# A hybrid GLA/HGRN2 diffusion step: each burst of the scan ordered behind a mark in the projection work

## The chip, the cores and the metric

The kernel runs on one core of one Trainium2 chip. The core has a matrix engine (TensorE, PE in the profile, with its weight loads as PEld), three engines for elementwise work (VectorE or DVE, ScalarE or ACT, GpSimd or POOL), a queue that issues transfers (SyncE, SP) and 16 DMA engines. Each engine works through its own queue of instructions in order and waits on semaphores for the others. The metric is the device time of one execution in microseconds; the median of several runs counts.

## The reference

One layer of a bidirectional backbone on 128 context tokens and 1024 latent tokens, width 1024, in float32:

```python
h = rmsnorm(x, norm1) * (1 + scale1) + shift1
mix, new_gla, new_hgrn = hybrid_mixer(h, s_gla, s_hgrn, w_in, w_gla_up, b_gla, lb, ...)
x = x + gate1 * mix
h = rmsnorm(x, norm2) * (1 + scale2) + shift2
x = x + gate2 * conv_ffn(h, w_ffn_up, ffn_conv, b_ffn_conv, w_ffn_down, grid)
```

The mixer projects h with `w_in` to queries, keys, values, gates and forget gates of 4 GLA heads (key width 64) and 4 HGRN2 heads (128), runs for each head a gated linear recurrence S_t = diag(f_t) S_{t-1} + k_t v_t^T, o_t = S_t^T q_t forward and backward over the tokens, adds both outputs, normalises them per head, multiplies by silu of a gate and projects with `w_out`. Modulation vectors come from `silu(c) @ w_ada`. The feed-forward part has a 3x3 depthwise convolution over the latent grid. Outputs are the two token tensors and the final states of the context.

## The kernel before

Large products run as three float32r products each (high times high, and the two with one low part), so every weight is split once: ACT writes the high part (`wh`, L127), POOL or DVE subtracts it to get the low part (`wl`, L65).

The first 750 us hold the mixer. The tokens are three blocks of 384; heads come in six groups: groups 0 and 1 are pairs of GLA heads, groups 2 to 5 one HGRN2 head each. Two streams of work share PE:

- *The scan* (`levels`). A block's intra-block scores are made by doubling: on levels 0 to 6 the decayed queries Q and keys k are updated in place by DVE (`update`, L886, L888, L892), ACT makes mixed copies of them (`mixed`, L876), and PE multiplies keys by queries in small 32-column products. One `burst` (L907 to L931) holds the products of two levels: 24 products, or 48 for a GLA pair, chained so that they go one behind the other, in float32, which the trace shows as two records each. A block has four bursts, a group 12, the scan 72. DVE picks the wanted parts of the PSUM result by a mask (`keep`). The next update of Q must wait until the burst has read it.
- *The fill* (`parts`, `all_steps`): all other projections of `w_in` in the order in which the groups need them (`proj_d_steps`, L598, 128 columns of weights against 384 tokens; `proj_t_steps`, L612, values, token-major), 2448 matmuls, and behind them `fill_steps`, the output projection of the first six token tiles over seven of the eight heads (L738, 252 matmuls). The memory of the normalised tokens is given back before `fill_steps`; its weights, the merged heads and a gate (L720) are loaded into that memory.

The main loop (L1185 to L1224) goes over groups, blocks and eight slots a block. Each even slot holds a burst, so a burst has an interval of two slots, and each slot has two parts. In every part the loop traces fill up to a planned number of columns (`goal`, from `GOALS`, with `D_COLS` = 27648 columns for one set of 128 weight columns); this fill is ordered behind the latest burst (`tc.issue_after(last.ins)`), in group 5 behind the latest state or output product (`anchor["mm"]`). In the same slots stand the steps of the block before: key transposes (`keys`, L984), state products (L991), and the outputs of the group before (`out_steps`: L1025 to L1028, L1051, L1065, turned by L1075), and, in groups 2 to 4, the products of the modulation (`ada_product`, L1152), whose weight pieces are loaded one interval ahead. `gates` (L818 to L857) prepares the next block; its `k` tile is one of two buffers.

The order on each queue is not written out: a planner in the framework simulates the engines with its own costs and takes, of the instructions that are ready in its simulation, the one that was traced first. `tc.high_priority(offset=BURST_AHEAD)` puts a burst 1000 instructions ahead in that rank, so a burst is taken as soon as its operands are ready there. `tc.issue_after(x)` adds an edge: the instructions traced in the block come behind x on x's engine, without waiting for its end. PSUM tiles of the fill (`ps_mm`) come in two buffers.

Behind the scan, from about 750 us, come the rest of the output projection, the feed-forward part with its convolution, and the down projection. The change does not touch them.

Of the kernel before, what the change touches and what calls it, by code (L numbers as in the profile page):

```python
# [49 lines left out]
def kernel(ctx: ExitStack, tc: tile.TileContext, ins, outs, stop=None):  # L50
# [9 lines left out]
    mm = nc.tensor.matmul  # L60

    anchor = {}
# [321 lines left out]
    for i in range(2):  # L384
        nc.vector.memset(modA[i], 0.0)
        t = modA[i][:, :]
# [7 lines left out]
    for i in range(2):  # L394
        ps = (ps_a, ps_mm)[i].tile([2 * 32, 512], F32, name="ada", tag=("ada", "mm")[i])
        psA.append(ps)
        for kt in range(KT):
# [4 lines left out]
            for j in range(2):  # L402
# [4 lines left out]
                    start=(kt == 0),  # L407
                    stop=(kt == KT - 1),
# [85 lines left out]
    def proj_d(w, b):  # L494

        hi, lo = w
        ps = ps_mm.tile([P, BL], F32, name="mm", tag="mm")
        n = 0
        for kt in range(KT):
            for a, h in ((hi, h1h), (hi, h1l), (lo, h1h)):  # L500
                mm(ps, a[:, kt, :], h[kt][b], start=(n == 0), stop=(n == 23))
                n += 1
        return ps

# [86 lines left out]
    def proj_d_steps(w, b, done):  # L591

        hi, lo = w
        ps = ps_mm.tile([P, BL], F32, name="mm", tag="mm")
        n = 0
        for kt in range(KT):
            for a, h in ((hi, h1h), (hi, h1l), (lo, h1h)):
                mm(ps, a[:, kt, :], h[kt][b], start=(n == 0), stop=(n == 23))  # L598
                n += 1
            if kt == KT - 1:  # L600
                done(ps)
            yield 3 * BL

    def proj_t_steps(w, t, done):

        ps = ps_mm.tile([P, 2 * P], F32, name="mm", tag="mm")
        ts_ = slice(t % 3 * P, (t % 3 + 1) * P)
        n = 0
        for kt in range(KT):
            hi, lo = w[kt // 4]  # L610
            for h, a in ((h1h, hi), (h1h, lo), (h1l, hi)):
                mm(ps, h[kt][t // 3][:, ts_], a[:, kt % 4, :], start=(n == 0), stop=(n == 23))  # L612
                n += 1
            if kt == KT - 1:
                done(ps)
            yield 3 * 2 * P
# [58 lines left out]
    def fill_steps():  # L675
# [14 lines left out]
        ws = list(next_ws(3))  # L690
# [32 lines left out]
        for b in range(2):  # L723
            if b == 1:
                ms = [load_merged(b, p) for p in range(3)]
            ms.append(load_merged(b, 3))
            for i in range(3):
                t = 3 * b + i
                xs = flat(vp.tile([P, NTILE, P], F32, name="v", tag="v"))
                nc.sync.dma_start(xs[:, 0:D], x_src(t))  # L730
                ts_ = slice(i * P, (i + 1) * P)
                for half in range(2):
                    cs = slice(half * 512, (half + 1) * 512)
                    ps = ps_mm.tile([P, 512], F32, name="mm", tag="mm")
                    for f in range(7):
                        for n, (a, wi) in enumerate(((0, 0), (0, 1), (1, 0))):
                            lhs = ms[f // 2][:, f % 2, a, ts_]
                            mm(ps, lhs, ws[f][wi][:, cs], start=(f + n == 0), stop=(f == 6 and n == 2))  # L738
                        if f == 6:
                            e = evp.tile([P, 512], F32, name="ev", tag="ev")  # L740
                            nc.vector.tensor_tensor(e, ps, gate[:, cs], op=ALU.mult)
                            nc.vector.tensor_tensor(e, e, xs[:, cs], op=ALU.add)
                            nc.gpsimd.dma_start(scr_pre[t][:, cs], e)
                        yield 3 * 512
                if t == 0:

                    cv = ins["ffn_conv"].rearrange("o a b (k p) -> (o a b k) p", p=P)
                    cr = flat(vp.tile([P, NTILE, P], F32, name="v", tag="v"))
                    nc.sync.dma_start(
                        cr[0:99, 0:512].rearrange("r (i p) -> r i p", i=4), cv.rearrange("(i r) p -> r i p", i=4)  # L750
                    )
                if t == 2:
                    for j in range(4):
                        pt = ps_x.tile([P, 512], F32, name="x", tag="x")
                        nc.tensor.transpose(pt[:, 0:99], cr[0:99, j * P : (j + 1) * P], ident[0:99, 0:99])
                        nc.vector.tensor_copy(conv_c[0][:, 99 * j : 99 * j + 99], pt[:, 0:99])
                if t == 4:
                    pos["end"] = n_in + 4
                    w_late.update({1: ws[1], 2: ws[2], 7: next_w()})
# [99 lines left out]
    def levels(u, b, fb, k, k0):  # L859
# [47 lines left out]
        def burst(*parts):  # L907

            widths = [LB << max(lev - NLOW, 0) for lev, _, _ in parts]
            pss = [ps_lv.tile([P, 3 * sum(widths)], F32, name="lv", tag="lv") for _ in u.heads]  # L910
            strips, at = [], 0
            for w in widths:
                strips.append([ps[:, at : at + 3 * w].rearrange("p (i n) -> p i n", i=3) for ps in pss])
                at += 3 * w
            last = None
            with tc.high_priority(offset=BURST_AHEAD):
                for (lev, keys, src), got in zip(parts[::-1], strips[::-1]):
                    for i in range(3):
                        for j in range(P // LB):
                            js = slice(j * LB, (j + 1) * LB)  # L920
                            for ps, (r0, r1) in zip(got, u.heads):
                                with tc.issue_after(last.ins) if last is not None else nullcontext():
                                    last = mm(  # L923
                                        ps[js, i, :],
                                        keys[r0:r1, i * P + j * LB : i * P + (j + 1) * LB],
                                        queries(lev, src, i, j, r0, r1),
                                        start=True,
                                        stop=True,
                                        skip_group_check=True,
                                    )  # L930
            return strips, last  # L931
# [182 lines left out]
    class Steps:  # L1114
# [12 lines left out]
        def drain(self):  # L1127
            while self.next is not None:
                self.step(self.next[0])
# [44 lines left out]
    def stream(goal, after):  # L1174
        nonlocal streamed
        while streamed < goal:
            with tc.issue_after(after.ins) if after is not None else nullcontext():
                got = next(steps, None)
            if got is None:
                return  # L1180
            streamed += got
# [3 lines left out]
    for n, u in enumerate(groups):  # L1185
        if not u.gla:
            u.v = [u.vpair[u.hd % 2]]
        if n == 0:
            start_group(u)
            ready = gates(u, 2)  # L1190
        for bi, b in enumerate(ORDER):
            fb, k, k0 = ready
            lv = levels(u, b, fb, k, k0)
            for slot in range(8):
                at = 8 * bi + slot
                last = anchor["mm"] = next(lv)
                if 2 <= n < 5 and slot % 2 == 0:
                    with tc.issue_after(last.ins):
                        with tc.high_priority(offset=BURST_AHEAD):
                            ada_product()  # L1200
                        ada_load()
                with tc.issue_after(last.ins):
                    outs_.step("half", at)
                    states.step("product")
                if slot == 5 and (b > 0 or n < 5):
                    if b > 0:
                        ready = gates(u, b - 1)
                    else:
                        start_group(groups[n + 1])
                        ready = gates(groups[n + 1], 2)  # L1210
                for part in range(2):
                    with tc.issue_after(last.ins):
                        if part == 0:
                            states.step("keys")
                        outs_.step("full", at)
                        if part == 1:
                            outs_.step("full", at)
                    goal = GOALS[n] + (GOALS[n + 1] - GOALS[n]) * (16 * bi + 2 * slot + part + 1) / 48
                    stream(goal, None if n == bi == 0 else anchor["mm"] if n == 5 else last)
            drain(lv)  # L1220
            states.drain()
            states = Steps(state_steps(u, b, k))
        outs_.drain()
        outs_ = Steps(out_steps(u))  # L1224
# [801 lines left out]
```

## Time and profile before

| | us |
|---|---|
| median of 3 runs | 1598.65 |
| lowest, highest | 1595.45, 1601.4 |
| profiled execution | 1602.16 |
| its span on the core | 1600.4 |
| PE busy | 1513.8 |
| DVE busy | 1160.1 |
| ACT busy | 793.1 |
| POOL busy | 726.4 |
| first and last burst start | 96.86, 688.97 |

The profiled execution is one run of the program under the hardware profiler; its time is 3.5 us above the median. Times inside the trace count from the start of the span. A matmul's record lasts longer than the distance to the next, since matmuls are pipelined: what PE loses shows as a stretch in which no record runs, put down as "idle before" with the engine that ended it. Bursts are counted here from 0 to 71, in the order of PE's queue.

### The profile page before, as it was taken

What the parts mean: (1) busy time and instruction counts of PE and PEld (TensorE: products, weight loads), DVE (VectorE), ACT (ScalarE), POOL (GpSimd) and SP (SyncE); (2) the same over time, 40 slices, a digit from 0 to 9 for tenths busy, and PEclk for the clock granted to TensorE, in tenths of its full rate; (3) what the DMA queues carried; (4) which work ended last, traced back from release to release, by engine and by line L of the source; (5) the groups of instructions that cost most, each with busy time, mean ns of one, the idle gap of its engine ahead of it and who ended that gap; (6) DMA issues with size and microseconds to landing.
All of it is one profiled execution on the core that took longest, in us unless ns stands there. A gap on an engine that the chain in (4) does not pass through costs nothing.

```text
span 1600.4 us, 31095 instructions
## 1 busy us (share of the span) xinstructions
PE 1513.8 (95%) x12506; PEld 1269.1 (79%) x12506; DVE 1160.1 (72%) x1724; ACT 793.1 (50%) x1526; POOL 726.4 (45%) x535
## 2 busy tenths in 40 slices
PE   7999998999999998799868999999999998999997
PEld 2699987989898988677656888888888886788886
DVE  3657563675575576544589999999999999678565
ACT  3566666545454455412664444444444444457444
POOL 1412122242432331201168999999999996200001
PEclk9999999999999999999979999999999999999999
DMA  9211111353544452644721464554554657879752
GB/s 334 100 56 46 38 46 52 104 148 121 168 138 133 141 174 92 257 165 152 259 72 40 132 191 131 135 142 122 176 139 111 186 137 212 320 232 356 254 187 116
DMA packets 164650, 244.61 MB, mean 153 GB/s; under 512 B 11124, under 2 KB 107618, under 8 KB 162586
## 3 DMA queue, kind: packets, MB, share of 16 engines
q1 hardware_dynamic: 142583, 168.54, 32.7%
q0 software_dynamic: 21312, 73.41, 15.1%
q8 instruction: 98, 1.61, 0.4%
q10 hardware_dynamic: 611, 0.68, 0.1%
q14 instruction: 46, 0.38, 0.1%
HBM read 186.95 MB, written 78.71 MB: 166 GB/s over the span
## 4 chain that ended last, share of the span: by engine, by line
PE 49%; DVE 6%; issue 2%; DMA 1%; ACT 1%; POOL 1%; POOLq 0%; SPq 0%; DVEq 0%; ACTq 0%
PE u L1477 25%; PE xb L1888 6%; PE yb L1888 5%; PE x L1682 4%; PE mm L738 3%; PE u L1370 2%; PE yb L1939 2%; DVE acc L1618 2%; PE x L1292 0%; DVE wl L65 0%; DMA scr_m<-hi 0%; DMA wh<-scr_wo 0%; DVE t4l L65 0%; DMA raw<-in_w_ffn_down_dram 0%; DMA mh<-scr_m 0%
## 5 line engine op out<-in xcount | busy, mean ns | idle before, releaser
L1618 DVE SCALAR_TENSOR_TENSOR acc<-u,convc,acc 128x945 f32<-128x945 f32 (+2 forms) x352 | 426.8, 1218 | 8.3 <-ACT acc L1606 1.8
L65 POOL TENSOR_TENSOR wl<-raw,wh 128x1024 fp32r<-128x1024 f32 x42 | 103.0, 2457 | 240.8 <-ACT wh L127 195.0
L598 PE MATMUL mm<-h1h,wh 128*128 128x384 f32 x528 | 185.5, 351 | 0.6 <-DVE g L647 0.6
L598 PE MATMUL mm<-h1h,wl 128*128 128x384 f32 x528 | 181.8, 344 | 0.0
L598 PE MATMUL mm<-h1l,wh 128*128 128x384 f32 x528 | 180.6, 342 | 0.0
L65 POOL TENSOR_TENSOR wul<-sr,wuh 128x512 fp32r<-128x512 f32 (+1 forms) x68 | 123.2, 1814 | 25.3 <-ACT wuh L1463 25.1
L65 POOL TENSOR_TENSOR wul<-ra,wuh 128x1024 fp32r<-128x1024 f32 x46 | 118.8, 2583 | 10.7 <-ACT wuh L1463 7.6
L886 DVE TENSOR_TENSOR Q<-Q,fb 128x384 f32<-128x384 f32 x126 | 80.4, 638 | 57.0 <-PE lv L923 55.6
L876 ACT ACTIVATE m<-k 128x384 f32<-128x384 f32 x126 | 70.2, 557 | 78.3 <-DVE k L888 38.3
L1863 POOL TENSOR_TENSOR sq<-sq,mhalf 128x1 f32<-128x1 f32 x9 | 11.1, 1238 | 213.9 <-DVE sq L1860 213.9
L598 PEld LDWEIGHTS mm<-h1h,wh 128*128 128x128 f32 x528 | 101.0, 191 | 4.3 <-issue 2.6
L598 PEld LDWEIGHTS mm<-h1h,wl 128*128 128x128 f32 x528 | 100.5, 190 | 2.2 <-issue 1.7
L598 PEld LDWEIGHTS mm<-h1l,wh 128*128 128x128 f32 x528 | 100.9, 191 | 1.1 <-issue 0.8
L888 DVE TENSOR_TENSOR k<-k,fb 128x384 f32<-128x384 f32 x126 | 76.4, 606 | 18.3 <-ACT m L876 10.3
L127 ACT ACTIVATE wh<-raw 128x1024 fp32r<-128x1024 f32 x55 | 58.1, 1057 | 54.2 <-DMA raw<-in_w_in_dram 14.8
L612 PE MATMUL mm<-wh,h1h 128*128 128x256 f32 x288 | 83.3, 289 | 0.0
L612 PE MATMUL mm<-wl,h1h 128*128 128x256 f32 x288 | 81.1, 282 | 0.0
L612 PE MATMUL mm<-wh,h1l 128*128 128x256 f32 x288 | 80.9, 281 | 0.0
L1463 ACT ACTIVATE wuh<-ra 128x1024 fp32r<-128x1024 f32 x44 | 46.4, 1054 | 38.0 <-issue 34.0
L1647 ACT ACTIVATE u2p<-u 128x512 f32<-128x512 f32 x44 | 26.3, 598 | 75.0 <-PE u L1477 71.8
L1714 POOL TENSOR_TENSOR acc<-acc,acc 128x1152 f32<-128x1152 f32 x22 | 59.6, 2711 | 6.9 <-DVE acc L1618 6.9
L1463 ACT ACTIVATE wuh<-sr 128x512 fp32r<-128x512 f32 (+1 forms) x66 | 51.0, 773 | 22.2 <-PE x L1682 16.2
(355 smaller groups left out, 4545.0 us busy)
## 6 DMA issues: line engine op xcount, KB each, us to landing
ra<-in_w_ffn_up_dram SPq DMA_DIRECT2D x88, 256.0 KB, 3.0
raw<-in_w_in_dram SPq DMA_DIRECT2D x32, 512.0 KB, 4.7
raw<-in_w_ada_dram SPq DMA_DIRECT2D x32, 512.0 KB, 4.1
scr_g<-acc POOLq DMA_DIRECT2D x22, 576.0 KB, 5.4
scr_s<-late POOLq DMA_DIRECT2D x11, 1024.0 KB, 4.2
scr_t<-in_w_ffn_down_dram POOLq DMA_DIRECT2D x16, 704.0 KB, 7.2
wa<-in_w_ada_dram SPq DMA_DIRECT2D x16, 512.0 KB, 6.4
raw<-in_w_out_dram SPq DMA_DIRECT2D x13, 512.0 KB, 3.6
```

What stands on the lines that cost most here:

```text
L65: return eng.tensor_tensor(out, full, hi.bitcast(F32), op=ALU.subtract)
L598: mm(ps, a[:, kt, :], h[kt][b], start=(n == 0), stop=(n == 23))
L612: mm(ps, h[kt][t // 3][:, ts_], a[:, kt % 4, :], start=(n == 0), stop=(n == 23))
L876: nc.scalar.activation(aps(t, 0, [[2 * h, NB], [h, 2], [1, h]]), aps(src, 0, [[2 * h, NB], [BL + h, 2], [1, h]]), AF.Copy)
L886: nc.vector.tensor_tensor(qm, qm, aps(ff_, 2 * h - 1, [[BL - h, 2], [2 * h, NB], [0, h]]), op=ALU.mult)
L888: nc.vector.tensor_tensor(km, km, aps(ff_, BL + 2 * h - 1, [[-(BL + h), 2], [2 * h, NB], [0, h]]), op=ALU.mult)
L1463: nc.scalar.activation(hi, raw, AF.Copy)
L1477: last = mm(dst, W[x][:, a, kt, :], HB[y][b][:, kt, :], start=(start and n == 0), stop=(stop and n == 11), skip_group_check=True,)
L1618: last = nc.vector.scalar_tensor_tensor(o, u3[:, r0 + dy : r1 + dy, c0 + dx : c1 + dx], wc(3 * (dy + 1) + dx + 1), o, op0=ALU.mult, op1=AL ...
L1682: last = mm(pk, HB[h]["p"][:, 4 * half + kt, :], aps(flat(W[x]), a * 512 + kt * P, [[(b - a) * 512, 2], [1, P]]), start=(half + kt + n == ...
L1714: last = nc.gpsimd.tensor_tensor(accg, accg, accu, op=ALU.mult)
L1888: anchor["down"] = mm(banks[i], w[a][:, ts_], w[b][:, 512:1024], start=(start and j == 0 and n == 0), stop=(j == NPAIR - 1 and n == 2), sk ...
```

## The change

Every matmul of the fill is noted as `anchor["fill"]` when it is traced. In the main loop, after the fill of the first part of an odd slot, which is the third of the four parts of an interval, the last fill matmul traced so far is noted as `anchor["paced"]`. The first product of the next burst, which until now had no ordering edge, is ordered behind that matmul; the other products of the burst are chained to the first as before. The priority of the burst, the fill's own edges and all data are the same.

```diff
@@ proj_d, proj_d_steps, proj_t_steps, fill_steps (each of the four fill matmuls)
-                mm(ps, a[:, kt, :], h[kt][b], start=(n == 0), stop=(n == 23))
+                anchor["fill"] = mm(ps, a[:, kt, :], h[kt][b], start=(n == 0), stop=(n == 23))
...
@@ burst
-            last = None
+            last = anchor.get("paced")
             with tc.high_priority(offset=BURST_AHEAD):
                 for (lev, keys, src), got in zip(parts[::-1], strips[::-1]):
...
@@ main loop
                     goal = GOALS[n] + (GOALS[n + 1] - GOALS[n]) * (16 * bi + 2 * slot + part + 1) / 48
                     stream(goal, None if n == bi == 0 else anchor["mm"] if n == 5 else last)
+                    if slot % 2 == 1 and part == 0:
+                        anchor["paced"] = anchor["fill"]
```

More of the change, by code (lines that the diff above doesn't have):

```diff
@@ L597, in proj_d_steps @@
             for a, h in ((hi, h1h), (hi, h1l), (lo, h1h)):
-                mm(ps, a[:, kt, :], h[kt][b], start=(n == 0), stop=(n == 23))
+                anchor["fill"] = mm(ps, a[:, kt, :], h[kt][b], start=(n == 0), stop=(n == 23))
                 n += 1
@@ L611, in proj_t_steps @@
             for h, a in ((h1h, hi), (h1h, lo), (h1l, hi)):
-                mm(ps, h[kt][t // 3][:, ts_], a[:, kt % 4, :], start=(n == 0), stop=(n == 23))
+                anchor["fill"] = mm(
+                    ps, h[kt][t // 3][:, ts_], a[:, kt % 4, :], start=(n == 0), stop=(n == 23)
+                )
                 n += 1
@@ L737, in fill_steps @@
                             lhs = ms[f // 2][:, f % 2, a, ts_]
-                            mm(ps, lhs, ws[f][wi][:, cs], start=(f + n == 0), stop=(f == 6 and n == 2))
+                            anchor["fill"] = mm(
+                                ps, lhs, ws[f][wi][:, cs], start=(f + n == 0), stop=(f == 6 and n == 2)
+                            )
                         if f == 6:
```

## The prediction

> **What bounds the kernel now.** First the page, then the waits of PE, then single stretches of PE's timeline. The page says PE 95%; the windows view splits the span into the first five groups of the scan, the last group with the tail, and everything behind the scan (length, busy time of PE, PEld, DVE, ACT, POOL, granted clock, DMA share, GB/s).
>
> ```profile
> span 1600.4 us, 31095 instructions
> PE 1513.8 (95%) x12506; PEld 1269.1 (79%) x12506; DVE 1160.1 (72%) x1724; ACT 793.1 (50%) x1526; POOL 726.4 (45%) x535
> 96.86:621.42 524.56, 506.34 (x7224) 464.10 (x7223) 320.77 (x696) 289.01 (x760) 146.92 (x127) 0.99 0.34 105
> 621.42:751.81 130.39, 113.94 (x1128) 95.73 (x1128) 66.80 (x169) 42.43 (x136) 19.56 (x27) 0.96 0.45 160
> 751.81:1600.40 848.59, 809.93 (x3743) 658.43 (x3741) 727.77 (x769) 414.82 (x542) 530.50 (x351) 0.98 0.56 176
> ```
>
> The change acts on the first two stretches. PE does the same matmuls before and after, so the change can only win or lose PE's idle time there: 524.56 - 506.34 = 18.2 us and 130.39 - 113.94 = 16.5 us. The waits view of PE says who ended it (us in total, times, longest); the first three rows are of the first stretch, the others of the whole span.
>
> ```profile
> PE lv L923 <- ACT m L876: 10.1, 5, 5.9
> PE ada L1152 <- DMA raw<-in_w_ada_dram: 4.3, 4, 1.2
> PE x L984 <- DVE st L1003: 2.0, 1, 2.0
> ...
> PE lv L923 <- ACT m L876: 14.9, 8, 5.9
> DVE Q L886 <- PE lv L923: 55.6, 42, 3.2
> ```
>
> L923 is the burst: eight of 72 bursts stop PE because their operand (L876) is late. The last row is the other direction: the scan's own engine waits for bursts, so the scan runs as fast as PE lets it.
>
> **Where the bursts stand now.** The new fence is the fill matmul that is last when the planner has traced three of four parts of an interval. In group n, burst j (0 to 11), the mark is GOALS[n] + (GOALS[n+1]-GOALS[n])*(4j-1)/48 columns, rounded up to a step of three matmuls. For group 2, j=11: 11.5+6.6*43/48 = 17.41 D_COLS; three v parts (216 matmuls each), eleven column parts (72 each) and 0.41*72 = 30 make 1470. The trace gives the fill actually issued: windows from 0 to a burst's start, of L598 alone and of L612 alone (matmul count in the second column).
>
> ```profile
> 0.00:391.54 391.54, 135.80 (x696) 121.33 (x696) 0.97 0.33 105
> 0.00:391.54 391.54, 83.48 (x648) 77.47 (x648) 0.97 0.33 105
> 0.00:272.93 272.93, 77.53 (x396) 68.63 (x396) 0.96 0.31 98
> 0.00:272.93 272.93, 55.75 (x432) 51.72 (x432) 0.96 0.31 98
> 0.00:557.33 557.33, 239.75 (x1241) 214.14 (x1241) 0.98 0.37 116
> 0.00:557.33 557.33, 111.56 (x864) 103.37 (x864) 0.98 0.37 116
> ```
>
> That burst goes at 696+648 = 1344, 126 before its mark. Done for all 72 bursts, 62 stand before their mark (9 to 60 matmuls mostly, up to 126) and move back; ten do not. Among the ten are two first bursts of a block: at 272.93 us the fill is at 828, which is all that is traced ahead of that burst, and at 557.33 at 2105 (mark 2106, limit 2112). So the scan runs ahead inside a block and then stands at the next block's start until the planned fill has caught up; a large stock of fill lies between. The edit takes the head start away and leaves PE at most a quarter interval, 9 to 15 matmuls, of fill that may go ahead of a late burst.
>
> **The change, part by part.** It adds no instruction; 62 ordering edges on PE's queue are what acts. The assignments to the anchor cost nothing. Behind a burst are queued its block's DVE updates and ACT copies, the ada products, the state and output products and the next fill, all fenced by it.
>
> 1. *Bursts that stop PE.*
>
> ```profile
> 212.54 0.77 PE L923 MATMUL lv<-Q,m 64*32 64x32 f32 x44 [1.93 <-ACT m L876]
> 272.93 0.71 PE L923 MATMUL lv<-Q,m 64*32 64x32 f32 x44 [5.91 <-ACT m L876]
> 432.09 0.40 PE L923 MATMUL lv<-Q,m 128*32 128x32 f32 x24 [1.68 <-ACT m L876]
> 656.20 0.34 PE L598 MATMUL mm<-h1l,wh 128*128 128x384 f32 x1
> 656.37 0.34 PE L598 MATMUL mm<-h1h,wl 128*128 128x384 f32 x1
> 212.70:216.11 3.41, 3.41 (x103) 3.35 (x102) 2.42 (x7) 1.89 (x3) 1.09 (x1) 0.50 0.02 5
> 605.23:608.64 3.41, 3.41 (x13) 3.41 (x13) 3.41 (x6) 1.43 (x5) 1.66 (x1) 0.50 0.39 115
> ```
>
> The bursts at 212.54 and 432.09 are 27 and 21 matmuls before their marks. A fill matmul goes every 0.17 us (the two L598 rows), so 4.6 and 3.6 us of fill go ahead of them, more than the 1.93 and 1.68 us they waited: 3.61 us gained. The one at 272.93 already stands at its limit; its 5.91 us stay. The last two rows (windows, granted clock in the third figure from the end) show that a stop also costs clock: 3.41 us at half rate follow the 1.93 us gap, and the same the 2.03 us gap at L984, so removing the first returns another 3.41/2 = 1.7. Term: -5.3 (bounds -5.3 and 0, if another burst inherits the wait).
> The Trainium skill ("TensorE: Matmul & The Clock Gate", Part 1: The HAM clock gate) has the clock fall after at least one idle window of about 3.4 us. By that rule a 1.93 us gap would cost only itself, the term would be -3.6 and the sum 1.7 us later; the row above disagrees, and I take the row.
>
> 2. *Ada products*.
>
> ```profile
> 343.15 0.64 PE L1152 MATMUL ada<-raw,cT 128*32 128x256 f32 x8 [1.23 <-DMA raw<-in_w_ada_dram]
> ```
>
> They (L1152) go right behind a burst and wait 4.3 us in four places for a piece whose load was issued one interval earlier. Even spacing helps where bursts stood close; but the wait shown, the longest, comes behind a burst that is 8.1 us after the one before it. I take half: -2.1 (bounds -4.3 and 0). The L984 gap of 2.0 us ends with a late state evacuation and is not touched: 0 (bounds -3.7 and 0).
>
> 3. *The change of stage in the last group.* Up to now bursts of group 5 fill PE while the output projection (L738) waits for its loads. Its mark for the first burst of block 1 is 2451, three matmuls past the last of the 2448 projection matmuls: that burst now waits for L738's first products, and the next (mark 2469) for the first seven weight pieces.
>
> ```profile
> 656.56 0.33 SPq L142 DMA_DIRECT2D wh<-scr_wo  x1
> 662.27 0.32 SPq L698 DMA_DIRECT2D mh<-scr_m  x1
> DMA  0000039955999999999999200000086030770999
> 669.11 0.48 PE L984 MATMUL x<-ident,k 128*128 128x128 f32 x1 [5.47 <-ACT st L995]
> 656.71:682.33 25.62, 14.89 (x197) 10.66 (x196) 14.45 (x38) 12.56 (x32) 5.39 (x8) 0.87 0.95 369
> 692.27 9.55 PE mm L738 x42
> 689.04 0.66 PE lv L923 x48
> 684.21 1.23 PE L991 MATMUL x<-v,kt 128*128 128x128 f32 x4 [0.89 <-ACT kt L987]
> ```
>
> The loads are issued from 656.56 (the last projection is done at 656.7) to 662.27, and the DMA slices of the window 640 to 715 (1.9 us each) stay full until about 682, 25.6 us later. In that stretch (656.71 to 682.33) PE is idle 25.62 - 14.89 = 10.7 us now, doing bursts, states and 24 L738 matmuls. With the fence it may do some 21 L738 matmuls (0.23 us each by the 42 in 9.55 us: 4.8), one burst (0.66), and gate, turn and state products that I put at 2.6 from the same timeline: 8.1, so 17.5 idle, 6.8 more. The gap of 0.89 us right behind it goes. Term: +6.0. Lower bound -4, if the loads land as fast and the 5.47 us stop, which is behind an ACT queue held by an output's DMA, goes too; upper bound +11.6, a second stop of that size. Behind it L738 is plentiful and PE full again.
>
> 4. *Block starts.*
>
> ```profile
> 551.60 0.27 PE L984 MATMUL x<-ident,k 128*128 128x128 f32 x1
> 552.08 0.52 ACT L852 ACTIVATE k<-fj 128x384 f32<-128x384 f32 x1
> 557.33 0.46 PE L923 MATMUL lv<-Q,m 128*32 128x32 f32 x24
> 426.30 2.88 DVE L864 TENSOR_TENSOR Q<-fb,qj 128x768 f32<-128x768 f32 x1 [2.31 <-ACT qj L510]
> 425.97 2.40 POOL L65 TENSOR_TENSOR wl<-raw,wh 128x1024 fp32r<-128x1024 f32 x1 [3.72 <-ACT wh L127]
> ...
> 607.69 0.56 DVE L888 TENSOR_TENSOR k<-k,fb 128x384 f32<-128x384 f32 x1
> 608.17 0.95 DVE L864 TENSOR_TENSOR Q<-fb,qj 128x768 f32<-128x768 f32 x1
> ```
>
> The first burst of a block follows the last key transpose of the block before last by 5.7 us, because L852 needs that k tile. Now ACT and DVE are free of the scan in that time; afterwards the block's own updates run there. An update is three DVE operations of about 0.56 us (607.69) and two lie in an interval: 3.3 us. Places within 4 matmuls or so of their limit now are few (182.5, 272.9, 557.3, 621.4 us); I take 0.75 us at each: +3.0. Bounds 0 and 4*3.3 = 13.2.
>
> Sum: -5.3 - 2.1 + 6.0 + 3.0 = +1.6 us. The profiled execution took 1602.16 us (span 1600.4), so 1603.8 by its own time; the median of the three runs shown is 3.5 lower, 1598.65, and gives 1600.
>
> **Rivals.** *Faster: the handover costs nothing.* For it: even intervals of (689.0-96.9)/71 = 8.3 us hold the 3.3 us of updates and three ACT copies with room, so a chip that runs later than the planner thought is covered at every burst. Terms: -5.3, -4.3, the L984 gap with its clock -3.7, the others 0: -13.3, 1585. Against it: the loads of the next stage cannot start before 2448 in either order.
> *Slower: PE runs dry at block starts.* With no stock of fill, each of the six starts that stand within 14 matmuls of their limit (118.3, 147.4, 182.5, 272.9, 557.3, 621.4 us) is late by the 3.3 us of updates, less the margin (0, 14, 3, 0, 7, 4 matmuls, 28*0.17 = 4.8): 19.8 - 4.8 = 15.0 in place of 3.0, so 1598.65 + 1.6 + 12 = 1612. It decides from a mean lateness of about 2.5 us a start. The pair of rows at 426 us speaks for it: a DVE step took 2.88 us while POOL was in a split; the same form took 0.95 us at 608.17. Against it: idle time at starts was small where the margin was large.
> The Trainium skill ("SBUF — State Buffer", SBUF: two separate sides) calls the port pair of DVE and GpSimd an exclusive lock, the loser blocked for the whole instruction. That pair of rows agrees.
> *The fence does nothing*: only if bursts already stood behind their marks, and 62 do not. 1599.
>
> **How the numbers follow.** Forecast 1600 (own range 1592 to 1608) 45%, handover free 1585 22%, starts dry 1612 31%, no effect 2%. A measurement tells about 0.5%, 8 us, from no change: below 1590.7 is faster, above 1606.6 slower. The forecast's ends give 3% faster and 5% slower, so 0.27, 0.37 and 0.36. Range 1584 to 1616: from the first rival to a little past the second, where terms 3 and 4 may both be at half their upper bounds.
>
> **What would show it.** Right: nearly all bursts at their marks; the waits PE lv on ACT m lose the 1.93 and 1.68 us entries; no L738 before, and one burst only, between the last projection and some 20 us later; DVE's wait for L923 grows well past 55.6 us. Wrong: the stretch behind the last projection stays at 10.7 us idle or less, the first bursts of blocks show new PE waits of 2 to 3 us at many places, or the stretch behind 751.81 changes length, on which nothing here acts.

## The result, and the profile after

The changed kernel took 1617.8 us (median of four runs, 1616.1 to 1619.2), the kernel before 1598.5 beside it (four runs, 1595.5 to 1601.4): a ratio of 1.0121, with a 95% interval from 1.0099 to 1.0142. It is slower, by 19 us. The prediction said 1600, with a range from 1584 to 1616. The profiled execution of the changed kernel took 1619.2 us, 1.4 above the median.

The head of its page, PE's waits between 180 and 780 us, and one row of DVE's waits (us in total, times, longest):

```profile
span 1617.3 us, 31087 instructions
PE 1514.2 (94%) x12506; PEld 1264.6 (78%) x12506; DVE 1149.6 (71%) x1724; ACT 800.1 (49%) x1530; POOL 727.7 (45%) x535
```

```profile
PE mm L598 <- ACT wh L127: 14.5, 3, 7.2
PE mm L740 <- DMA mh<-scr_m: 12.0, 5, 6.1
PE lv L927 <- ACT on L1039: 7.1, 1, 7.1
PE mm L598 <- POOL wl L65: 4.3, 3, 1.5
...
PE ada L1156 <- DMA raw<-in_w_ada_dram: 1.4, 2, 1.0
...
DVE Q L890 <- PE lv L927: 90.6, 48, 11.4
```

In this kernel L923, L984, L1152 and L738 of before are L927, L988, L1156 and L740; L598 kept its number. PE's busy time is what it was. Of the waits of bursts one long one is left, at k20 (7.1 us). New are the first and the fourth row: the *fill* stops, and it stops on its own weights. (The second row, 1.6 us in one wait before, belongs to the change of stage in the last group.) Twice the high part (ACT, L127) is about 7 us late, and each time the low part (POOL, L65) holds the third matmul another 1.4 us.

The windows view from the first burst to k20 (which in both kernels stands at fill 828), from there to k60 (fill 2345 before, 2349 after), and from k60 to the last fill matmul. First the kernel before, then the changed one; columns as in the prediction.

```profile
96.86:272.93 176.07, 166.89 (x2913) 152.69 (x2912) 103.15 (x246) 109.71 (x280) 33.76 (x27) 0.98 0.15 42
272.93:621.42 348.49, 339.45 (x4312) 311.40 (x4312) 217.62 (x451) 179.31 (x481) 113.16 (x101) 0.99 0.44 137
621.42:751.41 129.99, 113.54 (x1126) 95.42 (x1125) 66.80 (x169) 42.43 (x136) 19.56 (x27) 0.96 0.44 159
```

```profile
94.00:266.71 172.71, 163.24 (x2912) 149.29 (x2912) 102.13 (x244) 113.66 (x276) 32.49 (x25) 0.99 0.15 43
266.71:636.03 369.32, 345.35 (x4315) 314.32 (x4316) 206.19 (x453) 180.87 (x489) 115.60 (x102) 0.96 0.41 129
636.03:767.84 131.81, 115.53 (x1122) 94.33 (x1122) 68.57 (x169) 43.53 (x136) 18.48 (x27) 0.95 0.44 157
```

Up to k20 the changed kernel is 3.4 us faster, in the last group 1.8 slower, and in between it loses 20.8: its idle time there is 369.32 - 345.35 = 24.0 in place of 9.0, and the granted clock falls from 0.99 to 0.96. The sum, 19.3, is the whole loss. (The first burst starts 2.9 us earlier in this execution; it starts between 92.7 and 94.6 us in all the others, whatever their marks, so that is not an effect of the change.)

**What stops the fill.** The first stop on the queues of SP, ACT, POOL and PE (start, duration, and the idle time in brackets):

```profile
319.10 0.62 PE L1156 MATMUL ada<-raw,cT 128*32 128x256 f32 x6
319.75 0.34 SPq L126 DMA_DIRECT2D raw<-in_w_out_dram  x1
323.24 1.06 ACT L127 ACTIVATE wh<-raw 128x1024 fp32r<-128x1024 f32 x1 [0.36 <-DMA raw<-in_w_out_dram]
324.38 2.44 POOL L65 TENSOR_TENSOR wl<-raw,wh 128x1024 fp32r<-128x1024 f32 x1 [3.84 <-ACT wh L127]
326.85 9.73 SPq L126 DMA_DIRECT2D raw<-in_w_in_dram  x2
332.71 1.06 ACT L127 ACTIVATE wh<-raw 128x1024 fp32r<-128x1024 f32 x1 [5.48 <-DMA raw<-in_w_in_dram]
333.82 0.69 PE L598 MATMUL mm<-h1h,wh 128*128 128x384 f32 x1 [7.07 <-ACT wh L127]
336.25 0.69 PE L598 MATMUL mm<-h1h,wl 128*128 128x384 f32 x1 [1.42 <-POOL wl L65]
336.86 0.87 PE L927 MATMUL lv<-Q,m 128*32 128x64 f32 x24
337.85 1.06 PE L1156 MATMUL ada<-raw,cT 128*32 128x256 f32 x8
```

and the same loads before the change:

```profile
315.75 0.34 SPq L126 DMA_DIRECT2D raw<-in_w_out_dram  x1
320.18 0.66 PE L1152 MATMUL ada<-raw,cT 128*32 128x256 f32 x8
320.87 11.72 SPq L126 DMA_DIRECT2D raw<-in_w_in_dram  x3
327.78 1.06 ACT L127 ACTIVATE wh<-raw 128x1024 fp32r<-128x1024 f32 x1 [1.85 <-issue]
```

The pool `raw` has two buffers. Every weight piece to be split passes through it, and so does every piece of the modulation, which keeps its buffer until its ada product has run; that product stands behind a burst. At 319.7 the product behind k26 gives one buffer back. The other holds the next ada piece, whose product stands behind k27, and k27 now waits for fill matmul 1155. That is the third matmul of a projection that starts at 1152 and whose weight (`w_in`) is not loaded yet. So a piece of `w_out` and the weight PE needs go one after the other through one buffer: load, ACT, POOL, load, ACT, 14.1 us from the end of one product (319.72) to the first matmul (333.82). Fill matmuls 1096 to 1152 lasted until 326.75, and PE stood for the other 7.07 us. Before the change k26 and k27 went 75 and 105 matmuls earlier in the fill: the product behind k27 freed the second buffer at 320.84, the `w_in` load followed at 320.87, and nothing waited. The second stop is the same with k48, k49 (mark 2019) and the projection that starts at 2016.

The clock makes each stop larger. The windows of the changed kernel behind the first stop, and one behind a gap of 1.53 us that ends at 214.40 (granted clock in the third figure from the end):

```profile
333.82:337.23 3.41, 1.99 (x19) 1.15 (x23) 0.00 (x0) 0.00 (x0) 2.34 (x1) 0.50 0.00 0
337.23:340.64 3.41, 3.41 (x58) 2.60 (x51) 2.32 (x6) 0.90 (x2) 0.00 (x0) 0.52 0.78 181
340.64:344.05 3.41, 3.41 (x22) 3.41 (x21) 1.64 (x1) 2.62 (x5) 2.41 (x1) 1.00 0.48 132
214.40:217.81 3.41, 3.41 (x109) 3.08 (x110) 2.12 (x6) 2.70 (x11) 1.71 (x2) 1.00 0.58 159
```

Two stretches at half rate, with 1.99 and 3.41 us of work in them, cost about 2.6 us more by an estimate from these rows. The stop is 7.07 + 1.42 + 2.6 = 11.1 us, and two of them 22. The Trainium skill ("TensorE: Matmul & The Clock Gate", Part 1: The HAM clock gate) has the clock fall after at least one idle window of about 3.4 us. The 7.07 us stop and the stretches of 3.41 us agree with it; the 1.93 us gap of the kernel before, which was followed by 3.41 us at half rate, does not.

### The profile page after: what moved, and what is told of

Read it like the earlier page. It is cut to its first block, busy times and chain, and to the rows that moved or that the text cites. A ratio compares the mean times of both kernels' runs of the same rounds, so it can differ in the third digit from the quotient of the medians.

```text
span 1617.3 us, 31087 instructions
## 1 busy us (share of the span) xinstructions
PE 1514.2 (94%) x12506; PEld 1264.6 (78%) x12506; DVE 1149.6 (71%) x1724; ACT 800.1 (49%) x1530; POOL 727.7 (45%) x535
## 3 DMA queue, kind: packets, MB, share of 16 engines
q0 software_dynamic: 21312, 73.41, 14.7%
## 4 chain that ended last, share of the span: by engine, by line
PE 76%; DMA 8%; DVE 6%; ACT 4%; issue 3%; POOL 3%; SPq 0%; POOLq 0%; ACTq 0%; DVEq 0%
PE u L1483 25%; PE mm L598 12%; PE xb L1894 6%; PE mm L612 5%; PE yb L1894 5%; PE x L1688 4%; DMA raw<-in_w_in_dram 3%; PE mm L740 3%; PE lv L927 3%; PE yb L1945 2%; PE u L1376 2%; DVE acc L1624 2%; DMA mh<-scr_m 2%; POOL wl L65 1%; PE x L995 1%
## 5 line engine op out<-in xcount | busy, mean ns | idle before, releaser
L65 POOL TENSOR_TENSOR wl<-raw,wh 128x1024 fp32r<-128x1024 f32 x42 | 102.0, 2432 | 240.7 <-ACT wh L127 195.1
L598 PE MATMUL mm<-h1h,wh 128*128 128x384 f32 x528 | 188.3, 357 | 16.0 <-ACT wh L127 14.5
L598 PE MATMUL mm<-h1h,wl 128*128 128x384 f32 x528 | 181.8, 345 | 4.3 <-POOL wl L65 4.3
L598 PE MATMUL mm<-h1l,wh 128*128 128x384 f32 x528 | 180.4, 342 | 0.0
L890 DVE TENSOR_TENSOR Q<-Q,fb 128x384 f32<-128x384 f32 x126 | 82.5, 655 | 93.4 <-PE lv L927 90.6
L65 POOL TENSOR_TENSOR wul<-sr,wuh 128x512 fp32r<-128x512 f32 (+1 forms) x68 | 123.5, 1817 | 25.4 <-ACT wuh L1469 25.2
L65 POOL TENSOR_TENSOR wul<-ra,wuh 128x1024 fp32r<-128x1024 f32 x46 | 119.0, 2587 | 10.7 <-ACT wuh L1469 7.6
L598 PEld LDWEIGHTS mm<-h1h,wh 128*128 128x128 f32 x528 | 101.7, 193 | 22.5 <-ACT wh L127 15.4
L1869 POOL TENSOR_TENSOR sq<-sq,mhalf 128x1 f32<-128x1 f32 x9 | 11.1, 1237 | 214.7 <-DVE sq L1866 214.7
L598 PEld LDWEIGHTS mm<-h1h,wl 128*128 128x128 f32 x528 | 101.1, 192 | 7.1 <-POOL wl L65 5.6
L598 PEld LDWEIGHTS mm<-h1l,wh 128*128 128x128 f32 x528 | 101.4, 192 | 0.5 <-issue 0.3
L127 ACT ACTIVATE wh<-raw 128x1024 fp32r<-128x1024 f32 x55 | 58.1, 1057 | 68.7 <-DMA raw<-in_w_in_dram 32.4
L612 PE MATMUL mm<-wh,h1h 128*128 128x256 f32 x288 | 83.7, 291 | 0.0
L612 PE MATMUL mm<-wl,h1h 128*128 128x256 f32 x288 | 80.7, 280 | 0.0
L612 PE MATMUL mm<-wh,h1l 128*128 128x256 f32 x288 | 80.2, 279 | 0.0
```

Of the source, the lines that this page charges most:

```text
L65: return eng.tensor_tensor(out, full, hi.bitcast(F32), op=ALU.subtract)
L598: anchor["fill"] = mm(ps, a[:, kt, :], h[kt][b], start=(n == 0), stop=(n == 23))
L612: anchor["fill"] = mm(ps, h[kt][t // 3][:, ts_], a[:, kt % 4, :], start=(n == 0), stop=(n == 23))
L890: nc.vector.tensor_tensor(qm, qm, aps(ff_, 2 * h - 1, [[BL - h, 2], [2 * h, NB], [0, h]]), op=ALU.mult)
```

## The experiments

The theory after reading the two traces was H, the held buffer, as told above. Its rivals: A, the slower rival of the prediction (too little fill in hand at block starts); B, the change of stage in the last group; and M, that a mark just past the start of a projection stops PE whatever the buffers do. H was later put anew as H2.

`only2` comes to the kernel before with two marks added; all others are the changed kernel with the edit shown. Ratios are against the kernel before, on the same chip, with 95% intervals; "fill" is the number of fill matmuls issued.

### odd: ada steps in the other slots

```diff
-                if 2 <= n < 5 and slot % 2 == 0:
+                if 2 <= n < 5 and slot % 2 == 1:
```

> The changed kernel with the ada product and its load moved from the even slots of groups 2 to 4 to the odd ones, whose bursts get no mark; marks and everything else as changed. Theory H (held buffer): an ada piece keeps one of the two raw buffers until its product, the product stands behind a burst that now waits for a fill matmul, and that matmul needs a weight that must come through the other raw buffer; so both stops of 7 + 7 us (about 12 us each with the half-clock stretches behind them) go, and 1593 to 1597 us are left. Theory A (block starts run dry, the slower rival of the prediction): the stops come from too little fill in hand, the ada pieces have no part in it; about 1618. Theory B (the change of stage in the last group is what costs): about 1618 as well.

Measured: 1619.7 us, 1.0115 (1.0093 to 1.0137); the wait is still there:

```profile
PE mm L598 <- ACT wh L127: 14.7, 2, 7.5
```

The edit did not do what the expectation took it to do. In PE's order the products stand behind the same bursts as before (at fill 1035, 1095, 1155): a piece traced half an interval later is taken at the same place. So the run holds the pieces as long as the changed kernel does, and it tells nothing against any of the theories; it shows only that the time of an instruction is not where its line is.

### two: k27 and k49 without marks

```diff
-                    if slot % 2 == 1 and part == 0:
+                    if slot % 2 == 1 and part == 0 and (n, at) not in ((2, 5), (4, 1)):
```

> The changed kernel with two of its 27 marks left out: those of the bursts k27 and k49, the ones behind which the second ada piece of the interval stands and whose mark lies 3 matmuls into a projection whose weight is still to come. Theory H: these two waits alone close the ring, so both stops go: 1594 to 1598 us, and no 7 us wait of PE on the evictions of weights. Theory A: two bursts freed out of 27 change little, 1615 or more. Theory B: the last group's marks stand as they were, 1615 or more.

Measured: 1605.3 us, 1.0028 (1.0014 to 1.0042). (The marks are 72, one per burst, not 27.) PE's waits:

```profile
PE mm L598 <- ACT wh L127: 2.8, 2, 2.6
```

Two of 72 marks carry 15 of the 19 us. Theory A and theory B fall. But a wait of 2.6 us is left at the first place, and 7 us more than theory H left over.

### g01, g5 and g234: marks in some groups alone

```diff
-                    if slot % 2 == 1 and part == 0:
+                    if slot % 2 == 1 and part == 0 and n < 2:
...
+                    if slot % 2 == 1 and part == 0 and n == 5:
...
+                    if slot % 2 == 1 and part == 0 and 2 <= n < 5:
```

> Marks in groups 0 and 1 alone (no ada products and no change of stage lie there). Theory H with the prediction's first term: the bursts that stopped PE go and nothing is held, 1591 to 1594 us, 5 to 7 less than before. Theory A: the block starts of these groups are as tight as the later ones, so the fill runs dry here too: 1600 or more. Theory B: 1591 to 1594.

> Marks in the last group alone. Theory H with the prediction's third term: the change of stage costs its 6 us and the two stops are not there: 1602 to 1607 us. Theory B: the whole loss of the changed kernel is here, 1615 or more. Theory A: one of six groups, 1599 to 1603.

> Marks in groups 2 to 4 alone, where the ada pieces are. The runs with marks in groups 0 and 1 and in the last group gave -3.7 and +0.5 us against the kernel before, the whole change +18.4. If the effects add up: before plus about 21, 1618 to 1622, with both stops of PE. Theory A or B: 1605 or less, since the starts of other groups or the change of stage would carry the loss.

Measured: g01 1594.5 us, 0.9977 (0.9958 to 0.9995); g5 1601.4, 1.0003 (0.9990 to 1.0016); g234 1616.7, 1.0107 (1.0086 to 1.0128), with both stops:

```profile
PE mm L598 <- ACT wh L127: 14.2, 3, 7.1
```

Each of the three lies just outside the range that theory H gave (g01 0.5 us above it, g5 0.6 and g234 1.3 below). The loss sits in groups 2 to 4, where the ada pieces are, as theory H says; block starts of the same kind in groups 0 and 1 do not make g01 slower, and the change of stage alone costs nothing that can be measured. The three do not add up to the whole: -0.23 + 0.03 + 1.07 = 0.87% against 1.21%. The last group is why (below, at four_n5).

### skip: marks kept, two pieces loaded later

```diff
-                        ada_load()
+                        if (n, at) not in ((2, 4), (4, 0)):
+                            ada_load()
```

> The changed kernel, all marks kept, with two loads of ada pieces left out at their place and made up at the end of the list: those issued behind k26 and behind k48, so that no ada piece sits in a raw buffer while k27 and k49 wait for their marks (the same 32 pieces are loaded and multiplied, in the same order). Theory H (held buffer): the two waits of 7 us on the evictions of weights and the half-clock stretches behind them go, as where k27 and k49 lost their marks: 1602 to 1608 us, 10 to 15 less than the changed kernel. Theory A (too little fill in hand at starts): the pieces play no part, 1615 or more. Theory M (a mark just past the start of a projection stops PE whatever the buffers do, since its weight is loaded late): 1615 or more, with the waits at 326 and 540 us still there.

Measured: 1608.5 us, 1.0054 (1.0036 to 1.0072). The same row of PE's waits:

```profile
PE mm L598 <- ACT wh L127: 4.3, 3, 2.8
```

This is half a microsecond over what theory H allowed. Every mark is where it was and k27 and k49 wait for theirs, but the buffer that the piece of k27 held is free: the `w_out` load takes it at 310.60 and not at 319.75, and the 7 us waits are gone. So the held buffer is a cause, and theory M, that a mark just past the start of a projection stops PE whatever the buffers do, falls. Smaller waits stay: 2.8 us is the one at the second place.

### only2: the kernel before with marks for k27 and k49 alone

```diff
-                    if slot % 2 == 1 and part == 0:
+                    if slot % 2 == 1 and part == 0 and (n, at) in ((2, 5), (4, 1)):
```

> The kernel before with marks for k27 and k49 alone. Theory H: these two marks close the ring by themselves, PE stops twice and the time is 8 to 14 us over the kernel before (1608 to 1614). Theory A: two late bursts of 72 cost less than 3 us, 1598 to 1603. If the stops need the other marks too (the weight loads themselves pushed late by evenly spaced bursts), also 1598 to 1603.

Measured: 1595.6 us, 0.9970 (0.9958 to 0.9983): slightly *faster* than the kernel before, below every range above, and without either stop. (Of the gain 3.1 us lie in the last group, which took 126.9 us in place of 130.0.) Theory H as it was put falls: the two marks do not close the ring by themselves. k27 waits for fill 1155 here as well and holds its piece as long. What differs is k26: it goes at fill 1020, not 1095, so the serial way through the one free buffer starts 75 matmuls earlier (`w_out` at 313.46, `w_in` at 320.46) and is through in time.

### half: the mark at half of the interval

```diff
-                    if slot % 2 == 1 and part == 0:
+                    if slot % 2 == 0 and part == 1:
```

> The changed kernel with the mark at half of the planned fill of the interval in place of three quarters, in all groups. The marks of k27 and k49 are then 1140 and 2007, 12 and 9 matmuls ahead of the start of the next projection, so no weight stands between the burst and the release of its ada piece. Theory H: both 7 us stops go though the bursts are nearly as late and as even as before: 1598 to 1606. Theory A: a mark 12 matmuls earlier gives back at most half of the loss, 1608 or more.

Measured: 1609.5 us, 1.0065 (1.0041 to 1.0088). Half of the loss is gone, and yet the first stop is as long as in the changed kernel (timeline of SP and PE):

```profile
316.67 0.34 SPq L126 DMA_DIRECT2D raw<-in_w_out_dram  x1
324.58 1.34 SPq L126 DMA_DIRECT2D raw<-in_w_in_dram  x2
...
334.23 0.69 PE L598 MATMUL mm<-h1h,wh 128*128 128x384 f32 x1 [7.09 <-ACT wh L127]
```

The expectation of theory H fell here too, and the time lies where theory A put it, though two and g01 speak against A's reason. What only2 showed, that the start of the way at k26 counts, is seen here as well. k27 goes at 324.32 now, ahead of the stop, but that is when POOL's split frees the other buffer anyway; the `w_in` load cannot leave earlier than 324.58. The way from the product behind k26 (316.64) to the first matmul is 17.6 us; the 72 matmuls of fill that were left cover 10.5. The way starts earlier than in the changed kernel, but it is 3.5 us longer: most of that is the `w_in` load, which reaches ACT's split 8.5 us after its issue (333.12) and not 5.9; why it took longer is not shown. At the second place the stop is 3.95 us. So the theory was put anew (H2): what decides is the *length of the way through the buffers, from the burst that frees the first one*, against the fill left up to the projection that needs the weight.

### first: k26 and k48 without marks, k27 and k49 with them

```diff
-                    if slot % 2 == 1 and part == 0:
+                    if slot % 2 == 1 and part == 0 and (n, at) not in ((2, 3), (3, 23)):
```

> The changed kernel with the marks of k26 and k48 left out, those of k27 and k49 kept; k26 then goes behind matmul 1059 in place of 1095, k48 behind 1938 in place of 1971. Theory H2 (the length of the ring decides): behind k26's product come in series the load of one weight, its split, the load of the next projection's weight and its split, 14 us in the changed kernel's trace, while 57 matmuls of fill (about 10 us) are left up to the projection that needs it; starting 36 and 33 matmuls (6 us) earlier takes away most of each 7 us wait although k27 and k49 hold their pieces as long as before: 1604 to 1610 us, first waits at 2 us or less. Theory H as first put (the piece behind k27 and k49 alone decides): both 7 us waits stay, 1615 or more.

Measured: 1607.9 us, 1.0062 (1.0044 to 1.0080). A row of PE's waits, and the timeline of SP and PE at the first place:

```profile
PE mm L598 <- ACT wh L127: 5.9, 3, 3.2
```

```profile
315.34 0.34 SPq L126 DMA_DIRECT2D raw<-in_w_out_dram  x1
322.51 0.37 SPq L126 DMA_DIRECT2D raw<-in_w_in_dram  x1
...
329.71 0.64 PE L598 MATMUL mm<-h1h,wh 128*128 128x384 f32 x1 [2.42 <-ACT wh L127]
```

k27 is fenced as in the changed kernel and holds its piece, but the loads start 4.4 us earlier, and the wait falls from 7.07 to 2.42 us (a little over the 2 that were expected; at the second place 3.2). H2 holds, the first form of H does not. The "10 us" of the expectation was too much: 57 matmuls of L612 take 7.0 us.

### four, and four_n5

```diff
-                    if slot % 2 == 1 and part == 0:
+                    if slot % 2 == 1 and part == 0 and (n, at) not in ((2, 3), (2, 5), (3, 23), (4, 1)):
...
+                    if slot % 2 == 1 and part == 0 and n < 5 and (n, at) not in ((2, 3), (2, 5), (3, 23), (4, 1)):
```

> The changed kernel without the marks of k26, k27, k48 and k49; all others kept. If the ring is all that the change costs in groups 2 to 4, the two small stops that are left where only one of each pair is free (1.5 to 2.8 us, each with half-clock time behind it) go as well: 1598 to 1602 us, the level of the kernel before. If the even spacing itself costs the rest (about 7 us of the changed kernel's loss are still there with one of each pair free), 1604 or more.

> The changed kernel without the marks of k26, k27, k48 and k49 and without those of the last group. With the four marks out alone 4 us stayed over the kernel before. In the traces the last group (from k60 to the end of the fill) took 131 to 132 us where it had marks, 130.0 in the kernel before, and 125 to 127 in three runs with marks elsewhere only. If the rest of the loss sits there: 1595 to 1600 us, at or below the kernel before. If it sits in the earlier groups: 1602 or more.

Measured: four 1603.2 us, 1.0025 (1.0011 to 1.0038); four_n5 1597.0, 0.9980 (0.9966 to 0.9995). The windows of four, k20 to k60 and k60 to the end of the fill; below them the last stretch of four_n5, of g5 and of g01:

```profile
266.14:616.04 349.90, 340.34 (x4315) 310.82 (x4315) 205.46 (x453) 180.54 (x489) 114.67 (x102) 0.99 0.43 136
616.04:747.92 131.88, 115.85 (x1121) 94.78 (x1121) 68.54 (x169) 43.53 (x136) 18.49 (x27) 0.95 0.44 157
```

```profile
621.91:748.05 126.14, 114.74 (x1122) 96.08 (x1121) 66.64 (x169) 43.10 (x136) 18.93 (x27) 0.96 0.45 164
```

```profile
616.54:747.72 131.18, 114.84 (x1126) 94.30 (x1125) 68.50 (x169) 43.65 (x136) 18.54 (x27) 0.96 0.45 158
```

```profile
616.35:743.50 127.15, 112.41 (x1126) 95.14 (x1125) 66.64 (x169) 42.63 (x136) 18.80 (x27) 0.96 0.46 163
```

Without four of 72 marks the stretch from k20 to k60 is back at 349.9 us (369.3 with them, 348.5 before): nearly the whole loss there hung on two pairs of bursts. In four_n5, with the same marks up to k60, it took 353.4 us, and a stop on a weight is still there at the second place:

```profile
268.48:621.91 353.43, 342.80 (x4315) 313.34 (x4316) 206.67 (x453) 180.24 (x489) 115.55 (x102) 0.98 0.43 135
538.08 0.69 PE L598 MATMUL mm<-h1h,wh 128*128 128x384 f32 x1 [3.42 <-ACT wh L127]
```

In four the same stop is 2.01 us. In both, k48 goes at fill 1938 (1891 before), close behind k47, whose mark is 1923, so the way through the buffers still starts later than before the change. That the small stops go as well came true at the first place only, where no wait is over 0.7 us. Four took 1603.2, a little over the 1598 to 1602 that the first theory allowed. With the last group's marks off as well, it is at or just below the kernel before.

The last group: with marks it takes 131 to 134 us, with marks elsewhere only (g01, g234, only2, four_n5) 125 to 127, in the kernel before 130.0. So marks there cost about 5 us against the same group in a kernel with marks elsewhere, and about 1.5 against the kernel before, whose own order of that group is a poorer one. That is why the parts did not add up: g01 and g234 (125.1) each have an unmarked last group that is better than that of before. Why marks elsewhere give it a better order wasn't followed up.

A third raw buffer, the direct way to break the ring, wasn't tried, so what it would give is not shown.

## Why the prediction was wrong

- **Where the bursts stand: right.** From k5 to k54 every burst stands at its mark or within 9 matmuls behind it, in even steps of mostly 7 to 10 us; DVE's wait for bursts grew from 55.6 to 90.6 us, as forecast.
- **Bursts that stop PE (-5.3): direction right, size -3.4, but not by less idle time.** Both waits of bursts are gone from the list. Up to k20 eight kernels with these marks took 172.7 to 174.6 us, four without them 176.1 to 176.4. But part of the wait was inherited, by the fill: a product of L598 now stands 1.53 us until DVE is done with a gate (L649; the fill has two PSUM buffers, and L649 reads one). PE's idle time up to k20 did not fall at all, 9.5 us in place of 9.2 (172.71 - 163.24 and 176.07 - 166.89); the same matmuls kept PE busy 3.65 us less, at a clock of 0.99 in place of 0.98. The half-rate stretch that the prediction named is 1.7 of that; where the rest lies is not shown. And the clock is not sure to be won: in two and four_n5 a gap of 1.54 us at this place was followed by a clock of 0.74 over 3.41 us, and these two are the slowest of the eight, 174.3 and 174.6 us.

```profile
214.40 0.45 PE L598 MATMUL mm<-h1h,wh 128*128 128x384 f32 x1 [1.53 <-DVE g L649]
214.65:218.06 3.41, 3.41 (x104) 3.10 (x105) 2.13 (x6) 2.70 (x11) 1.71 (x2) 0.74 0.60 159
```

  (The first row is of the changed kernel, the second of four_n5.) At the second place, 432 us, a gap of 1.48 us, for a weight's low part, took the place of 1.68.
- **Ada products (-2.1, bounds -4.3 and 0): the step that failed.** Their own wait fell from 4.3 to 1.4 us, more than the half that was forecast and within the bounds. What the step left out is that an ada product that moves back with its burst keeps one of two raw buffers, and that SP's loads of the *fill's* weights queue behind that buffer. Only PE's waits were costed for the moved step; SP's queue and the buffer's other users were not named. The ring that came of it (the burst waits for fill, the fill for a weight, the weight for a buffer, the buffer for a burst's product) cost two stops of 11 us. The upper bound of 0 for this term had no row behind it. The rows for it were there: the L65 and L1152 rows that the prediction quotes both read `raw`, and the marks 1155 and 2019, three matmuls into a projection, follow from the same formula that the prediction used for 2451 in the last group.
- **The change of stage (+6.0): right sign, wrong working.** In the 25.62 us behind the last projection PE was to be idle 17.5 us:

```profile
666.71:692.33 25.62, 14.71 (x98) 9.70 (x96) 5.70 (x16) 4.43 (x11) 2.68 (x5) 0.80 0.98 386
```

  It was idle 25.62 - 14.71 = 10.9, against 10.7 before: practically what the prediction named as the sign that this step is wrong. With 27 L740 matmuls begun (21 were forecast), one burst and a clock of 0.80, PE was busy for 14.7 us and not 8.1. The group as a whole took 1.8 us longer than before, and g5 measured 1.0003; the cost of 5 us that the comparison of four and four_n5 shows is against another order of the group.
- **Block starts (+3.0): about +1.2.** Only k20 changed, from 5.91 to 7.11 us; no new waits of 2 to 3 us at first bursts. So the slower rival, 1612, was nearest in time and wrong in its reason: PE did run dry, but not for bursts, and not at block starts.
- **Stock of fill.** The prediction saw that the head start of the scan goes and asked only what the *bursts* lose by it. The head start was also what gave raw buffers back in time: before the change k27's product went 102 matmuls ahead of the projection whose load needed its buffer.

## What to carry to other kernels

When an edge moves an instruction back, list what its operands hold (here one of two buffers) and who else needs that, down to the loads on the DMA queues; an edge from stream A to stream B closes a ring as soon as B's inputs pass through a buffer that A gives back. The price is then the length of the serial way through the buffer less the work left to cover it, plus the clock lost behind the stop, and it falls in a few places only: four marks of 72 made the whole stretch slow. The even spacing of the bursts was worth the 3.4 us up to k20, and behind k20 no run shows a gain from it.

## What had not been expected of the hardware

The length of a gap in PE's work does not settle what it costs in clock. In the changed kernel a gap of 1.53 us left the clock at 1.00, in four_n5 one of 1.54 at the same place was followed by 0.74 over 3.41 us. In the kernel before one of 1.93 us was followed by 3.41 us at half rate, and a longer one, 2.45 us (the burst at 636.83), was not:

```profile
636.83:640.24 3.41, 3.41 (x79) 3.12 (x83) 3.41 (x12) 1.28 (x2) 0.00 (x0) 1.00 0.02 5
```

So the two gaps from which the prediction took its clock term were not the whole picture; what decides is not shown. The stop of 7.07 us with one of 1.42 behind it was followed by two slow stretches. The way of a weight through its raw buffer is not of one length either: from the issue of a `w_in` piece to ACT's split it took 5.9 us in the changed kernel (326.85 to 332.71), 6.9 in the kernel before (320.87 to 327.78) and 8.5 in half (324.58 to 333.12).
